# First attention of the second block: a pair's logits as one alternating run, the second pair of a step one projection tile later

## The chip, the core and the metric

The kernel runs on one core of a Trainium2 chip. The metric is the device time of one execution in microseconds (us), lower is better; the kernel before takes 1923.35 us (median of 3 runs, 1921.4 to 1927.18).

## The reference

The program computes two transformer blocks on one sequence of 512 tokens of width 1024, in float32. The first block is a gated delta net beside a retention mixer and a convolutional MLP. The second block has two layers, each an attention and a squared-ReLU MLP; the change lies in the attention of its first layer. Cut to what matters there:

```python
A_GROUPS = ((128, 1, 6), (512, 4, 5), (2048, 16, 5))     # window, dilation, heads
def dilated_window_attention(xn, w_qkv, w_o, rel_bias):  # 16 heads of 64
    q, k, v = split(xn @ w_qkv)                          # q scaled by 64 ** -0.5
    for (win, dil, nh) in A_GROUPS:
        n_side = win // (2 * dil)                        # 64 keys on either side, dil apart
        logits = q . k over the window + bias            # -inf outside the sequence
        lse = logsumexp(logits); p = exp(logits - lse); o = p . v
        glses.append(logsumexp(lse over the group's heads) - log(nh))
    alpha = softmax(glses)                               # one weight per token and group
    return concat(o * 3 * alpha) @ w_o
```

## The kernel before, in words

Activations are held with features on the 128 partitions and the 512 tokens along the free axis, as 8 tiles. Every projection of a layer is made of tiles of 128 output features: `project` issues 24 matmuls of 512 columns for one tile (8 slices of the contraction, 3 products of a high and a low half of weights and activations). They write a tile `ps_pj` of PSUM; VectorE evacuates it. The weights come by DMA in blocks of two tiles (`raw`), ScalarE copies their high half (`hi`, L251) and VectorE takes the rest (`lo`, L252). TensorE (PE), VectorE (DVE) and ScalarE (ACT) each run their own instructions in order.

`layer_a` (L988) works through a table of steps, `A_STEPS` (L26). Step numbers 0 to 3 each stand for four heads, that is two pairs: `q0`, `k0`, `v0` are two projection tiles each, `s0` the logits and the softmax of the four heads, `t0` the transposes of their probabilities, `p0` the products with v. After `s0` stands `v0` (two tiles), then `t0`; after `s1`, `s2` and `s3` stand `v1`, `q3` and `v2`, then `t1`, `t2` and `t3`. `a0` makes the weights of the three groups from all heads' minima `MN` and sums `SS`; it begins with 12 matmuls `ps_bc`.

The two heads of a pair lie in one tile of q and k, the first on partitions 0 to 63, the second on 64 to 127. A head's logits are 4 matmuls with a contraction of 64, one per block `j` of 128 queries. In the first group (heads 0 to 5) they have 192, 256, 256 and 192 columns, and two blocks share a PSUM tile `ps_lg`; in the other groups (heads 6 to 15) they have 128 columns, and all four blocks share one. The trace shows each of these float32 matmuls as two, called passes here: 128 for 64 instructions. For each block VectorE adds the bias and takes the minimum (L1083, the negated logits are kept), and ScalarE takes the exponential with its sum (L1085); per head follow a reciprocal (L1087) and the normalisation (L1090). `softmax_head` writes this block by block: matmul, addition, exponential, next block. The probabilities of the first group take one of 3 buffers `P` per head, those of the others one per pair. PSUM tiles other than `ps_pj` come from a pool `pw` of 5.

The order on each engine is made by a list scheduler when the program is built, from the order of the code, the dependencies and its own estimates; `chain` and `in_order` pin one instruction behind another. `M_["pe"]` is the last projection matmul written.

Of the kernel before, what the change touches and what calls it, by code (L numbers as in the profile page):

```python
# [9 lines left out]
F32 = mybir.dt.float32  # L10
F32R = mybir.dt.float32r
AF = mybir.ActivationFunctionType
ALU = mybir.AluOpType
# [3 lines left out]
P = 128  # L17
T = 512
# [5 lines left out]
A_GROUP = [0] * 6 + [1] * 5 + [2] * 5  # L24
# [145 lines left out]
def build(nc, tc, a, out, phases=("mix", "mlp1", "A", "mlpA", "B", "mlpB")):  # L170
# [12 lines left out]
    act = nc.scalar.activation  # L183
    V = nc.vector
    G = nc.gpsimd

    def mm(o, l, r, start=True, stop=True):
        return nc.tensor.matmul(o, lhsT=l, rhs=r, start=start, stop=stop)  # L188
# [8 lines left out]
    def in_order(i1, i2):  # L197
        tc.add_manual_dep(i2.ins, i1.ins.name, mybir.DependencyInfo(
            mybir.DependencyClass.NoSync, mybir.DependencyReason.DATA))
# [5 lines left out]
    def chain(insts):  # L205
        for x, y in zip(insts, insts[1:]):
            in_order(x, y)

    def pwt(name, shape=None):
        return pw.tile(shape or [P, T], F32, tag="w", name=name)  # L210
# [75 lines left out]
    M_ = {}  # L286
# [92 lines left out]
    def project(pieces, x, n=T, cols=P):  # L379

        if pre:
            return pre.pop(0)
        ps = pj.tile([P, T], F32, tag="pj", name="ps_pj")[0:cols, 0:n]
        nk = len(x)
        for k in range(nk):
            hi, lo = pieces[k // KD]
            M_["pe"] = mm3(ps, (hi[:, k % KD, 0:cols], lo[:, k % KD, 0:cols]), x[k], k == 0, k == nk - 1)
        return ps
# [86 lines left out]
    def mixer(st):  # L475
# [8 lines left out]
        def unit(tag, bufs, name, dt=F32, shape=None):  # L484
            pool = lp if tag == "L" else gp
            return pool.tile(shape or [P, T], dt, tag=tag, name=name, bufs=bufs)
# [79 lines left out]
        def stage_a(hh):  # L566
            H = HD[hh]
            kT, KQ, vT = H["kT"], H["KQ"], H["vT"]

# [12 lines left out]
            V.tensor_scalar(out=rq, in0=rq, scalar1=128 ** -0.5, scalar2=None, op0=ALU.mult)  # L582
            H["rq"] = rq
            brk = sp.tile([P, 4], F32, tag="brk", name="brk")
# [22 lines left out]
            G.tensor_tensor(out=qd, in0=KQ[:, 1, :], in1=er, op=ALU.mult)  # L607
            H["qd"] = qd
            kbe = unit("L", NL, "kbe")
            G.tensor_tensor(out=kbe, in0=KQ[:, 0, :], in1=er, op=ALU.mult)  # L610
            H["kbe"] = kbe
            N = unit("L", NL, "N")
            QE = unit("L", NL, "QE")
            for c2 in range(2):
# [6 lines left out]
                for aa, (o_, m_) in enumerate(((N, E2), (QE, E))):  # L621
                    V.tensor_tensor(out=o_[:, cs].rearrange("p (c i) -> p c i", c=2), in0=pg[:, :, aa, :],
                                    in1=m_[:, cs].rearrange("p (c i) -> p c i", c=2), op=ALU.mult)
            H["N"], H["QE"] = N, QE
            nc.sync.dma_start(d1[hh], N.rearrange("p (c i) -> p c i", c=4))
# [363 lines left out]
    def layer_a(st, biasd):  # L989
        x = st.x  # L990
# [3 lines left out]
        gp = tmpc.__enter__()  # L994
        b1 = gp.tile([P, 6, 256], F32, name="b1")
        b2 = gp.tile([P, 5, P], F32, name="b2")
        b3 = gp.tile([P, 5, P], F32, name="b3")
# [9 lines left out]
        MN = gp.tile([P, 16, 4], F32, name="MN")  # L1007
        SS = gp.tile([P, 16, 4], F32, name="SS")
        RC = gp.tile([P, 16, 4], F32, name="RC")
# [23 lines left out]
        def evac(ps, m, scale, dst, ordf):  # L1033
            gs = (A_GROUP[2 * m], A_GROUP[2 * m + 1])
            parts = [(slice(0, P), gs[0])] if gs[0] == gs[1] else [(slice(0, 64), gs[0]), (slice(64, P), gs[1])]
            for sl, g in parts:
                i = V.tensor_tensor(out=ordf(g, dst[sl, :]), in0=nat(g, ps[sl, :]), in1=nat(g, scale[sl, :]), op=ALU.mult)
            return i
# [11 lines left out]
            for c in range(4):  # L1050
                V.tensor_copy(b3[32 * c:32 * c + 32, :, 96 - 32 * c:128 - 32 * c], b3t[32 * c:32 * c + 32])

        PP = {}

        def softmax_head(hh, q, k):
            g = A_GROUP[hh]
            pr = slice(64 * (hh % 2), 64 * (hh % 2) + 64)
            W = 256 if g == 0 else P
            if g == 0:
                pt = gp.tile([P, 4, W], F32, tag="P", name="pt", bufs=3)  # L1060
            else:
                if hh % 2 == 0:
                    PP[hh // 2] = gp.tile([P, 2, 4, W], F32, tag="P", name="pt", bufs=3)
                pt = PP[hh // 2][:, hh % 2]
            H = dict(P=pt, rng=[])
            for j in range(4):
                if g == 0:
                    if j % 2 == 0:
                        lg = pwt("ps_lg").rearrange("p (j x) -> p j x", j=2)
                    k0, k1 = max(0, P * j - 64), min(T, P * j + 192)  # L1070
                    x0 = k0 - (P * j - 64)
                    x1 = x0 + k1 - k0
                    lj = lg[:, j % 2, x0:x1]
                    bias = b1[:, hh, x0:x1]
                else:
                    if j == 0:
                        lg = pwt("ps_lg").rearrange("p (j x) -> p j x", j=4)
                    k0, k1, x0, x1 = P * j, P * j + P, 0, P
                    lj = lg[:, j, :]
                    bias = (b2[:, hh - 6, :] if g == 1 else b3[:, hh - 11, :])  # L1080
                H["rng"].append((x0, x1))
                mm(lj, q[pr, P * j:P * j + P], k[pr, k0:k1])
                V.tensor_tensor_reduce(out=pt[:, j, x0:x1], in0=lj, in1=bias, scale=1.0, scalar=3e38,  # L1083
                                       op0=ALU.add, op1=ALU.min, accum_out=MN[:, hh, j:j + 1])
                act(out=pt[:, j, x0:x1], in_=pt[:, j, x0:x1], func=AF.Exp, scale=-1.0, bias=MN[:, hh, j:j + 1],  # L1085
                    accum_out=SS[:, hh, j:j + 1])
            V.reciprocal(out=RC[:, hh, :], in_=SS[:, hh, :])  # L1087
            for j0, j1, x0, x1 in ((0, 1, 64, 256), (1, 3, 0, 256), (3, 4, 0, 192)) if g == 0 else ((0, 4, 0, P),):
                ap = pt[:, j0:j1, x0:x1]
                V.tensor_tensor(out=ap, in0=ap, in1=RC[:, hh, j0:j1].unsqueeze(2).to_broadcast([P, j1 - j0, x1 - x0]),  # L1090
                                op=ALU.mult)
            return H

        def vtiles(m, vT):

# [100 lines left out]
        def proj(m0, nm):  # L1196
            wb = ws.take()
            r = []
            for i in range(2):
                ps = project(wb[i:i + 1], x)  # L1200
                t = gp.tile([P, T], F32, tag=nm, name=nm, bufs=2)
                M_["evac"] = evac(ps, m0 + i, rs8 if nm == "q" else st.rs, t, rorder if nm == "q" else order)
                r.append(t)
            return r

        def parts_of(m):
# [26 lines left out]
        M_["evac"] = None  # L1233
        oT, HS, qv, kv, vv = {}, {}, {}, {}, {}

        def soft_pairs(i2):
            for i in range(2):
                m = 2 * i2 + i
                HS[m] = [softmax_head(2 * m + e, qv[i2][i], kv[i2][i]) for e in range(2)]

        def turn_pairs(i2):
            for hh in range(4 * i2, 4 * i2 + 4):
# [13 lines left out]
        for step in A_STEPS:  # L1256
            nm, i2 = step[0], int(step[1])
            if step == "q1":
                load_third_bias()
            if step == "q2":  # L1260
                third_bias()
            if nm in "qkv":
                {"q": qv, "k": kv, "v": vv}[nm][i2] = proj(2 * i2, nm)
            elif nm == "s":
                soft_pairs(i2)
            elif nm == "t":
                turn_pairs(i2)
            elif nm == "p":
                pv_pairs(i2)
            else:  # L1270
                alphas()
                for m in range(4):
                    weigh(m, lambda g, sl: nat(g, oT[m][sl, :]))
# [328 lines left out]
```

## Time and profile before

| | |
|---|---|
| median of 3 runs | 1923.35 us |
| profiled execution, its own time | 1921.55 us |
| span of the profiled execution, first to last instruction | 1919.7 us |
| mean granted TensorE clock | 0.997 of full speed |
| PE busy | 1885.3 us, 98% |
| DVE, ACT, GpSimd busy | 1109.8, 766.1, 143.3 us |
| first and last logits matmul of this attention start at | 727.5 and 859.4 us |

In a page's or a view's rows, PE is a matmul on TensorE, PEld a load of its weights, and "out<-in" names the tiles. A row of the timeline gives the start in us, the time from the first start to the last end, the engine, the line and the operation, and how many instructions it merges (x4). Matmuls overlap in time, so the distance of two starts is what one costs a busy PE, and not its duration.

### The profile page before, as it was taken

Reading aid. Unit: us, or ns where it says so; the run is one execution under the profiler, and the core shown is the slowest. Engines: PE = TensorE matmul, PEld = TensorE weight load, DVE = VectorE, ACT = ScalarE, POOL = GpSimd, SP = SyncE. Lnnn points to the kernel's source line nnn. Section 1 sums busy time; section 2 is a strip of 40 time slices with the busy share of each in tenths; the row PEclk is TensorE's granted clock in tenths of the full one; section 3 lists DMA queues with packets and bytes.
Section 4 is the critical chain, followed back from the end, with each engine's and each line's share of the span. In section 5 each row is a group of like instructions: output and inputs, shape, how many; then the busy total and the mean of one; then the engine's idle time right before and its main releaser. Section 6 shows DMA issues by size and latency. Waiting matters only on the chain.

```text
span 1919.7 us, 23518 instructions
## 1 busy us (share of the span) xinstructions
PE 1885.3 (98%) x9219; PEld 1545.1 (80%) x9219; DVE 1109.8 (58%) x2109; ACT 766.1 (40%) x1350; POOL 143.3 (7%) x136
## 2 busy tenths in 40 slices
PE   7999999999999999999999999999999999999997
PEld 5887878788888887777888888888888888888886
DVE  7795756666356575558544344447877754334433
ACT  5523334343234444345342133336656543213322
POOL 1231210011001002000000000001111000000000
PEclk9999999999999999999999999999999999999999
DMA  5231213222322234112323222333222232222321
GB/s 191 79 116 56 74 45 121 95 88 88 110 103 86 76 112 160 64 52 99 110 89 109 88 106 92 111 131 135 95 73 101 81 112 88 97 101 89 109 88 44
DMA packets 39646, 185.53 MB, mean 97 GB/s; under 512 B 9055, under 2 KB 10847, under 8 KB 22000
## 3 DMA queue, kind: packets, MB, share of 16 engines
q1 hardware_dynamic: 37552, 177.45, 26.3%
q0 software_dynamic: 1984, 6.59, 1.0%
q8 instruction: 72, 1.18, 0.2%
q14 instruction: 38, 0.31, 0.1%
HBM read 176.31 MB, written 7.71 MB: 96 GB/s over the span
## 4 chain that ended last, share of the span: by engine, by line
PE 55%; DVE 3%; ACT 1%; issue 1%; DVEq 0%; ACTq 0%
PE ps_pj L188 49%; PE ps_ob L188 1%; PE ps_lgb L188 1%; PE ps_po L188 1%; PE ps_aT L1380 1%; PE ps_lg L188 1%; ACT junk L1397 0%; PE ps_bc L188 0%; DVE KL L1337 0%; DVE lo L252 0%; DVE nb L408 0%; DVE nb L409 0%; PE ps_obT L1409 0%; PE ps_pT L1140 0%; PE ps_mean L188 0%
## 5 line engine op out<-in xcount | busy, mean ns | idle before, releaser
L188 PE MATMUL ps_pj<-xh,hi 128*128 128x512 f32 x1504 | 592.2, 394 | 10.2 <-ACT hi L251 9.3
L188 PE MATMUL ps_pj<-xl,hi 128*128 128x512 f32 x1504 | 591.7, 393 | 0.0
L188 PE MATMUL ps_pj<-xh,lo 128*128 128x512 f32 x1504 | 590.9, 393 | 0.0
L251 ACT ACTIVATE hi<-raw 128x1024 fp32r<-128x1024 f32 (+2 forms) x308 | 317.2, 1031 | 649.1 <-PE ps_pj L188 611.0
L252 DVE TENSOR_TENSOR lo<-raw,hi 128x1024 fp32r<-128x1024 f32 (+2 forms) x308 | 369.6, 1202 | 300.2 <-ACT hi L251 299.2
L188 PEld LDWEIGHTS ps_pj<-xh,hi 128*128 128x128 f32 x1504 | 283.1, 188 | 69.0 <-ACT hi L251 9.8
L188 PEld LDWEIGHTS ps_pj<-xh,lo 128*128 128x128 f32 x1504 | 283.1, 188 | 58.1 <-DVE lo L252 1.1
L188 PEld LDWEIGHTS ps_pj<-xl,hi 128*128 128x128 f32 x1504 | 283.1, 188 | 57.6 <-DVE xl L280 0.6
L188 PE MATMUL ps_pj<-ah,lo 128*128 128x512 f32 (+1 forms) x704 | 271.0, 385 | 0.0
L188 PE MATMUL ps_pj<-al,hi 128*128 128x512 f32 (+1 forms) x704 | 270.7, 385 | 0.2 <-DVE al L277 0.2
L188 PE MATMUL ps_pj<-ah,hi 128*128 128x512 f32 (+1 forms) x704 | 270.9, 385 | 0.0
L188 PEld LDWEIGHTS ps_pj<-al,hi 128*128 128x128 f32 x704 | 132.3, 188 | 26.9 <-DVE al L277 0.5
L188 PEld LDWEIGHTS ps_pj<-ah,hi 128*128 128x128 f32 x704 | 132.3, 188 | 26.4 <-ACT ah L276 0.4
L188 PEld LDWEIGHTS ps_pj<-ah,lo 128*128 128x128 f32 x704 | 132.3, 188 | 25.9
L469 DVE TENSOR_TENSOR ot<-ps_pj,r 128x512 f32<-128x512 f32 x31 | 21.5, 692 | 108.1 <-PE ps_pj L188 108.1
L188 PE MATMUL ps_pj<-mh,hi 128*128 128x512 f32 x192 | 74.9, 394 | 1.0 <-ACT mh L276 0.9
L276 ACT ACTIVATE ah<-ms 128x512 fp32r<-128x512 f32 x64 | 40.4, 632 | 87.4 <-DVE ms L974 85.9
L188 PE MATMUL ps_pj<-ml,hi 128*128 128x512 f32 x192 | 74.4, 392 | 0.6 <-DVE ml L277 0.6
L188 PE MATMUL ps_pj<-mh,lo 128*128 128x512 f32 x192 | 74.0, 390 | 0.0
L277 DVE TENSOR_TENSOR al<-ms,ah 128x512 fp32r<-128x512 f32 x64 | 44.3, 693 | 45.0 <-ACT ah L276 45.0
L947 DVE SCALAR_TENSOR_TENSOR my<-ms,cols,my 128x511 f32<-128x511 f32 (+1 forms) x88 | 65.6, 748 | 2.8 <-ACT my L945 1.3
L1364 ACT ACTIVATE Lb<-Lb,bmn 128x512 f32<-128x512 f32 x64 | 45.6, 714 | 13.9 <-DVE bmn L1362 11.6
(341 smaller groups left out, 1895.9 us busy)
## 6 DMA issues: line engine op xcount, KB each, us to landing
raw<-w_all SPq DMA_DIRECT2D x137, 1024.0 KB
bt<-biasd SPq DMA_DIRECT2D x16, 448.0 KB
raw<-w_all SPq DMA_DIRECT2D x8, 768.0 KB
raw<-w_all SPq DMA_DIRECT2D x8, 640.0 KB
hscr<-h POOLq DMA_DIRECT2D x16, 256.0 KB, 2.5
hold<-hscr SPq DMA_DIRECT2D x16, 256.0 KB
hs<-x_t SPq DMA_DIRECT2D x8, 256.0 KB
hold<-x_t SPq DMA_DIRECT2D x8, 256.0 KB
```

The lines of the kernel that those rows point to most:

```text
L188: return nc.tensor.matmul(o, lhsT=l, rhs=r, start=start, stop=stop)
L251: act(out=hv, in_=iv, func=AF.Copy)
L252: i_lo = V.tensor_tensor(out=lv, in0=iv, in1=hv.bitcast(F32), op=ALU.subtract)
L276: act(out=dst_hi, in_=src, func=AF.Copy)
L277: V.tensor_tensor(out=dst_lo, in0=src, in1=dst_hi.bitcast(F32), op=ALU.subtract)
L469: V.tensor_tensor(out=t, in0=ps, in1=scale_row, op=ALU.mult)
L947: V.scalar_tensor_tensor(out=y[:, jj:], in0=s[:, :T - jj], scalar=col(base + m), in1=y[:, jj:], op0=ALU.mult, op1=ALU.add)
L1364: act(out=L, in_=L, func=AF.Exp, scale=-1.0, bias=mn[:, j, t:t + 1], accum_out=ss[:, j, t:t + 1])
L1380: nc.tensor.transpose(ps[:, t * P:(t + 1) * P], A[t][:, kt * P:(kt + 1) * P], ident)
```

## The change

`softmax_head` is replaced by `softmax_pair`, for both heads of a pair. It writes the matmuls of the two heads in turn (block 0 of the first head, block 0 of the second, block 1 of the first, ...), chains them, pins the first of them behind the last projection matmul, and writes the additions and exponentials behind the matmuls of the two PSUM tiles that they read, one per head. The second pair of a step is not issued at `s`: it is kept in `second` and issued by `proj` after the next projection tile. No operand, shape, number of instructions or DMA changes.

```diff
-        def softmax_head(hh, q, k):
+        def softmax_pair(m, q, k):
+            g = A_GROUP[2 * m]
             W = 256 if g == 0 else P
+            nj = 2 if g == 0 else 4
...
-            for j in range(4):
...
-                mm(lj, q[pr, P * j:P * j + P], k[pr, k0:k1])
-                V.tensor_tensor_reduce(out=pt[:, j, x0:x1], in0=lj, in1=bias, scale=1.0, scalar=3e38,
-                                       op0=ALU.add, op1=ALU.min, accum_out=MN[:, hh, j:j + 1])
-                act(out=pt[:, j, x0:x1], in_=pt[:, j, x0:x1], func=AF.Exp, scale=-1.0, bias=MN[:, hh, j:j + 1],
-                    accum_out=SS[:, hh, j:j + 1])
+            before = M_["pe"]
+            for j0 in range(0, 4, nj):
+                lg = [pwt("ps_lg").rearrange("p (j x) -> p j x", j=nj) for _ in range(2)]
+                todo, seq = [], []
+                for j in range(j0, j0 + nj):
...
+                    for e in range(2):
+                        hh = 2 * m + e
+                        pr = slice(64 * e, 64 * e + 64)
...
+                        lj = lg[e][:, j - j0, x0:x1]
+                        Hs[e]["rng"].append((x0, x1))
+                        seq.append(mm(lj, q[pr, P * j:P * j + P], k[pr, k0:k1]))
+                        if before is not None:
+                            in_order(before, seq[0])
+                            before = None
+                        todo.append((hh, j, pts[e][:, j, x0:x1], lj, bias))
+                chain(seq)
+                for hh, j, pj_, lj, bias in sorted(todo, key=lambda t: t[:2]):
+                    V.tensor_tensor_reduce(out=pj_, in0=lj, in1=bias, scale=1.0, scalar=3e38,
+                                           op0=ALU.add, op1=ALU.min, accum_out=MN[:, hh, j:j + 1])
+                    act(out=pj_, in_=pj_, func=AF.Exp, scale=-1.0, bias=MN[:, hh, j:j + 1],
+                        accum_out=SS[:, hh, j:j + 1])
...
                 M_["evac"] = evac(ps, m0 + i, rs8 if nm == "q" else st.rs, t, rorder if nm == "q" else order)
                 r.append(t)
+                if second:
+                    soft_pair(*second.pop())
...
+        second = []
+
+        def soft_pair(i2, i):
+            HS[2 * i2 + i] = softmax_pair(2 * i2 + i, qv[i2][i], kv[i2][i])
+
         def soft_pairs(i2):
-            for i in range(2):
-                m = 2 * i2 + i
-                HS[m] = [softmax_head(2 * m + e, qv[i2][i], kv[i2][i]) for e in range(2)]
+            soft_pair(i2, 0)
+            second.append((i2, 1))
```

What this does to the order is shown at three places. The first is PE at step `s0`, where the first pair's logits stand. `q_5949` and `k_6013` are the first pair's q and k. Before, heads 0 and 1 have the PSUM tiles 6043, 6050 and 6062, 6069 (blocks 0 and 1, blocks 2 and 3); what stands in brackets is the engine whose counter the matmul waits for:

```order
L188 MATMUL ps_lg_6043<-k_6013,q_5949 128x192 [waits DVE_49]
L188 MATMUL ps_lg_6050<-k_6013,q_5949 128x256
L188 MATMUL ps_lg_6062<-k_6013,q_5949 128x192 [waits PE_49]
L188 MATMUL ps_lg_6069<-k_6013,q_5949 128x256 [waits Activation_49]
L188 MATMUL ps_lg_6043<-k_6013,q_5949 128x256 [waits DVE_49]
L188 MATMUL ps_lg_6050<-k_6013,q_5949 128x192 [waits DVE_49]
L188 MATMUL ps_lg_6062<-k_6013,q_5949 128x256 [waits DVE_49]
L188 MATMUL ps_lg_6069<-k_6013,q_5949 128x192 [waits DVE_49]
```

The same place in the changed kernel; the tiles are 6044, 6058 (head 0) and 6045, 6059 (head 1), and `ps_pj_6090` is the first tile of `v0`:

```order
L188 MATMUL ps_lg_6044<-k_6013,q_5949 128x192 [waits DVE_49]
L188 MATMUL ps_lg_6045<-k_6013,q_5949 128x192
L188 MATMUL ps_lg_6044<-k_6013,q_5949 128x256
L188 MATMUL ps_lg_6045<-k_6013,q_5949 128x256
L188 MATMUL ps_lg_6058<-k_6013,q_5949 128x256 [waits PE_49]
L188 MATMUL ps_lg_6059<-k_6013,q_5949 128x256 [waits Activation_49]
L188 MATMUL ps_lg_6058<-k_6013,q_5949 128x192
L188 MATMUL ps_lg_6059<-k_6013,q_5949 128x192
L188 MATMUL ps_pj_6090<-xh0_5425,hi_5980 128x512 [waits PE_49]
```

The waits of the second half for VectorE are gone, the two heads alternate, and projection matmuls follow at once, where before the second pair's logits followed.

The second place is PE at step `s3`, heads 12 to 15 (128 columns). Before, the logits of both pairs (`q_6898` and `q_6925`) mix with each other and with the first projection matmuls of `v2` (`ps_pj_7091`):

```order
L188 MATMUL ps_lg_7020<-k_6990,q_6898 128x128 [waits DVE_49]
L188 MATMUL ps_pj_7091<-xh0_5425,lo_6958 128x512
L188 MATMUL ps_lg_7035<-k_6990,q_6898 128x128 [waits DVE_49]
L188 MATMUL ps_lg_7051<-k_7017,q_6925 128x128 [waits DVE_49]
L188 MATMUL ps_pj_7091<-xh1_5477,hi_6957 128x512
L188 MATMUL ps_lg_7066<-k_7017,q_6925 128x128 [waits DVE_49]
L188 MATMUL ps_pj_7091<-xl1_5478,hi_6957 128x512
L188 MATMUL ps_pj_7091<-xh1_5477,lo_6958 128x512
L188 MATMUL ps_pj_7091<-xh2_5530,hi_6957 128x512
L188 MATMUL ps_lg_7066<-k_7017,q_6925 128x128 [waits DVE_49]
```

Changed, the second pair's run stands whole between the 24 matmuls of the first tile of `v2` (`ps_pj_7060`) and the 24 of the second (`ps_pj_7118`), after which the transposes of `t3` come:

```order
L188 MATMUL ps_pj_7060<-xh7_5795,lo_6958 128x512
L188 MATMUL ps_lg_7088<-k_7017,q_6925 128x128 [waits DVE_49,Activation_49]
L188 MATMUL ps_lg_7089<-k_7017,q_6925 128x128 [waits Activation_49]
L188 MATMUL ps_lg_7088<-k_7017,q_6925 128x128
L188 MATMUL ps_lg_7089<-k_7017,q_6925 128x128
L188 MATMUL ps_lg_7088<-k_7017,q_6925 128x128
L188 MATMUL ps_lg_7089<-k_7017,q_6925 128x128
L188 MATMUL ps_lg_7088<-k_7017,q_6925 128x128
L188 MATMUL ps_lg_7089<-k_7017,q_6925 128x128
L188 MATMUL ps_pj_7118<-xh0_5425,hi_6961 128x512 [waits PE_49]
```

All eight of a pair's matmuls now stand together, and the two logits runs of a step are 24 projection matmuls apart.

The third place is VectorE at the same step, from the first reciprocal on. Before (`pt_7019` are the probabilities of heads 12 and 13, `pt_7050` those of 14 and 15; `v_7116` is the evacuation of the first tile of `v2`):

```order
L1087 RECIPROCAL RC_5905<-SS_5904 128x4 [waits Activation_49]
L1083 ISA pt_7050,MN_5903<-ps_lg_7066,b3_5898 128x128 [waits PE_49]
L1083 ISA MN_5903 128x1
L1090 TENSOR_TENSOR pt_7019<-pt_7019,RC_5905 128x512 [waits DVE_49]
L1087 RECIPROCAL RC_5905<-SS_5904 128x4 [waits Activation_49]
L252 TENSOR_TENSOR lo_7084<-raw_7081,hi_7083 128x1024 [waits DMAHW2_49]
L1090 TENSOR_TENSOR pt_7050<-pt_7050,RC_5905 128x512 [waits DVE_49]
L1087 RECIPROCAL RC_5905<-SS_5904 128x4 [waits Activation_49]
L252 TENSOR_TENSOR lo_7088<-raw_7081,hi_7087 128x1024
L1090 TENSOR_TENSOR pt_7050<-pt_7050,RC_5905 128x512 [waits DVE_49]
L1037 TENSOR_TENSOR v_7116<-ps_pj_7091,rs_5864 128x128x4 [waits PE_49]
```

Changed (`pt_7087` are heads 14 and 15, `v_7085` is the first tile of `v2`):

```order
L1096 RECIPROCAL RC_5905<-SS_5904 128x4 [waits Activation_49]
L252 TENSOR_TENSOR lo_7057<-raw_7050,hi_7056 128x1024
L1099 TENSOR_TENSOR pt_7019<-pt_7019,RC_5905 128x512 [waits DVE_49]
L1096 RECIPROCAL RC_5905<-SS_5904 128x4 [waits Activation_49]
L1099 TENSOR_TENSOR pt_7019<-pt_7019,RC_5905 128x512 [waits DVE_49]
L1037 TENSOR_TENSOR v_7085<-ps_pj_7060,rs_5864 128x128x4 [waits PE_49]
L1090 ISA pt_7087,MN_5903<-ps_lg_7088,b3_5898 128x128 [waits PE_49]
L1090 ISA MN_5903 128x1
```

The second pair's additions now come behind the evacuation of the first tile of v, where before they were mixed with the first pair's.

## Rows read from the trace of the kernel before

**Rows 1.** The page: span, and busy time by engine with share and instructions.
```profile
span 1919.7 us, 23518 instructions
PE 1885.3 (98%) x9219; PEld 1545.1 (80%) x9219; DVE 1109.8 (58%) x2109; ACT 766.1 (40%) x1350; POOL 143.3 (7%) x136
```

**Rows 2.** The logits' tile ps_lg: instructions, then idle time before them by releaser.
```profile
L188 PE MATMUL ps_lg<-k,q x128: 269/323/480, 727.5 to 859.4; 64*128 64x128 f32 x80, 64*128 64x192 f32 x24, 64*128 64x256 f32 x24
...
  DVE MN L1083: 6.5, 19
```

**Rows 3.** Stretches around logits (start:end, length, busy by engine, PEclk), first, some, last.
```profile
727.17:732.14 4.97, 4.57 (x29) 3.01 (x28) 4.55 (x20) 4.68 (x13) 3.06 (x4) 1.00 1.06 390
733.99:735.16 1.17, 1.17 (x5) 0.59 (x4) 1.17 (x5) 1.07 (x5) 0.00 (x0) 1.00 0.12 39
...
852.53:853.60 1.07, 1.07 (x7) 0.60 (x6) 0.65 (x1) 0.82 (x1) 0.00 (x0) 1.00 0.00 0
853.60:858.59 4.99, 4.71 (x32) 3.25 (x30) 3.97 (x33) 4.62 (x23) 0.00 (x0) 1.00 0.01 2
858.82:859.90 1.08, 1.08 (x6) 0.59 (x4) 0.76 (x5) 1.08 (x7) 0.00 (x0) 1.00 0.05 15
sum 31.85, PE 30.51 PEld 19.11 DVE 26.54 ACT 26.82 POOL 3.06; mean PE 2.03 PEld 1.27 DVE 1.77 ACT 1.79 POOL 0.20
```

**Rows 4.** Chain of waits: two projection tiles without anything between.
```profile
842.02 10.91 PE ps_pj L188 x48
```

**Rows 5.** Timeline of PE at step s3.
```profile
852.85 0.49 PE L188 MATMUL ps_lg<-k,q 64*128 64x128 f32 x4
...
857.84 0.49 PE L188 MATMUL ps_lg<-k,q 64*128 64x128 f32 x2
```

**Rows 6.** Timeline of PE at step s0: wider logits.
```profile
731.17 0.70 PE L188 MATMUL ps_lg<-k,q 64*128 64x256 f32 x4 [0.31 <-DVE MN L1083]
...
734.30 0.59 PE L188 MATMUL ps_lg<-k,q 64*128 64x192 f32 x2
```

**Rows 7.** Timeline of PE: a pair's products with v, two heads in turn.
```profile
812.92 0.40 PE L188 MATMUL ps_pj<-xh,hi 128*128 128x512 f32 x1
813.25 1.09 PE L188 MATMUL ps_po<-pT,vt 128*64 128x128 f32 x16
814.27 0.50 PE L188 MATMUL ps_pj<-xl,hi 128*128 128x512 f32 x1
814.60 0.39 PE L188 MATMUL ps_pj<-xh,lo 128*128 128x512 f32 x1
```

**Rows 8.** Timeline of PE, 727.4 to 728.4 us: the first eight logits passes.
```profile
727.49 1.03 PE L188 MATMUL ps_lg<-k,q 64*128 64x192 f32 x8
```

**Rows 9.** Timeline of VectorE at step s3: the four heads' softmax.
```profile
853.89 0.27 DVE L1083 CUSTOM_DVE_ANT_0 pt<-ps_lg,b 128x128 f32<-128x128 f32 x1
...
862.38 1.19 DVE L252 TENSOR_TENSOR lo<-raw,hi 128x1024 fp32r<-128x1024 f32 x1
863.49 0.69 DVE L1090 TENSOR_TENSOR pt<-pt,RC 128x512 f32<-128x512 f32 x1
864.09 1.09 DVE L1037 TENSOR_TENSOR v<-ps_pj,rs 128x512 f32<-128x512 f32 x1
865.01 0.18 DVE L1167 TENSOR_REDUCE mg<-MN 128x4 f32<-128x20 f32 x1
```

**Rows 10.** Timeline of ScalarE: the sums' logarithm in step a0.
```profile
867.01 0.21 ACT L1174 ACTIVATE sg<-sg 128x12 f32<-128x12 f32 x1
```

**Rows 11.** Timeline of PE at steps t3 and a0.
```profile
868.77 0.39 PE L188 MATMUL ps_pj<-xh,lo 128*128 128x512 f32 x1
869.00 1.91 PE L1140 MATMUL ps_pT<-ident,pt 128*128 128x128 f32 x16
870.74 2.84 PE L188 MATMUL ps_bc<-ident,sg 128*128 128x128 f32 x24
```

**Rows 12.** Timeline of PE at step t0: the smaller runs of transposes.
```profile
744.82 0.47 PE L188 MATMUL ps_pj<-xh,hi 128*128 128x512 f32 x1
745.26 0.66 PE L1129 MATMUL ps_pT<-ident,pt 128*128 128x128 f32 x4
745.67 0.48 PE L188 MATMUL ps_pj<-xl,hi 128*128 128x512 f32 x1
```

**Rows 13.** Waits on PE that stand behind step a0.
```profile
PE ps_pj L188 <- ACT mh L276: 0.9, 1, 0.9
PE ps_pj L188 <- DVE ml L277: 0.6, 1, 0.6
```

**Rows 14.** Timeline of PE's weight loads where the tile shape changes.
```profile
762.72 0.20 PEld L188 LDWEIGHTS ps_po<-pT,vt 64*64 64x64 f32 x4 [0.17 <-issue]
```

More of the change, by code (lines that the diff above doesn't have):

```diff
@@ L1051, in third_bias @@
                 V.tensor_copy(b3[32 * c:32 * c + 32, :, 96 - 32 * c:128 - 32 * c], b3t[32 * c:32 * c + 32])
-        PP = {}
-        def softmax_head(hh, q, k):
-            g = A_GROUP[hh]
-            pr = slice(64 * (hh % 2), 64 * (hh % 2) + 64)
+        def softmax_pair(m, q, k):
+            g = A_GROUP[2 * m]
             W = 256 if g == 0 else P
+            nj = 2 if g == 0 else 4
             if g == 0:
-                pt = gp.tile([P, 4, W], F32, tag="P", name="pt", bufs=3)
+                pts = [gp.tile([P, 4, W], F32, tag="P", name="pt", bufs=3) for _ in range(2)]
@@ L1061, in softmax_head @@
             else:
[L1062 to L1065, printed above, removed]
-            for j in range(4):
[L1067 to L1071, printed above, removed]
-                    x1 = x0 + k1 - k0
[L1073 to L1081, printed above, removed]
-                mm(lj, q[pr, P * j:P * j + P], k[pr, k0:k1])
-                V.tensor_tensor_reduce(out=pt[:, j, x0:x1], in0=lj, in1=bias, scale=1.0, scalar=3e38,
-                                       op0=ALU.add, op1=ALU.min, accum_out=MN[:, hh, j:j + 1])
-                act(out=pt[:, j, x0:x1], in_=pt[:, j, x0:x1], func=AF.Exp, scale=-1.0, bias=MN[:, hh, j:j + 1],
-                    accum_out=SS[:, hh, j:j + 1])
@@ L1087, in softmax_head @@
[L1087 to L1092, printed above, removed]
+                pt2 = gp.tile([P, 2, 4, W], F32, tag="P", name="pt", bufs=3)
+                pts = [pt2[:, e] for e in range(2)]
@@ new lines, in softmax_pair @@
+            Hs = [dict(P=pts[e], rng=[]) for e in range(2)]
+            before = M_["pe"]
[3 more added lines that the diff above has]
+                for j in range(j0, j0 + nj):
+                    if g == 0:
+                        k0, k1 = max(0, P * j - 64), min(T, P * j + 192)
+                        x0 = k0 - (P * j - 64)
+                    else:
+                        k0, k1, x0 = P * j, P * j + P, 0
+                    x1 = x0 + k1 - k0
+                    for e in range(2):
+                        hh = 2 * m + e
+                        pr = slice(64 * e, 64 * e + 64)
+                        gh = A_GROUP[hh]
+                        bias = b1[:, hh, x0:x1] if gh == 0 else b2[:, hh - 6, :] if gh == 1 else b3[:, hh - 11, :]
+                        lj = lg[e][:, j - j0, x0:x1]
[11 more added lines that the diff above has]
+                        accum_out=SS[:, hh, j:j + 1])
@@ new lines, in softmax_pair @@
+            for e in range(2):
+                hh, pt = 2 * m + e, pts[e]
+                V.reciprocal(out=RC[:, hh, :], in_=SS[:, hh, :])
+                for j0, j1, x0, x1 in ((0, 1, 64, 256), (1, 3, 0, 256), (3, 4, 0, 192)) if g == 0 else ((0, 4, 0, P),):
+                    ap = pt[:, j0:j1, x0:x1]
+                    V.tensor_tensor(out=ap, in0=ap,
+                                    in1=RC[:, hh, j0:j1].unsqueeze(2).to_broadcast([P, j1 - j0, x1 - x0]), op=ALU.mult)
+            return Hs
```

## The prediction

> **What bounds the kernel.** I first read the page's engine times: PE is busy for 1885.3 of 1919.7 us, VectorE for 58% and ScalarE for 40% [rows 1]. The reader is to see there that only time taken from PE's own stream shortens the program. Then the view of the tile ps_lg: this attention's logits are 128 passes of 64 rows, and PE's side sat idle for 6.5 us in front of them, in 19 places, until VectorE had read an earlier block [rows 2]. That is little, so I asked what the logits cost PE in all. I cut 15 stretches out of the trace, each from the last projection matmul before some logits to the second one after them; together they hold all 128 passes and take 31.85 us [rows 3]. Most hold two projection matmuls, the stretch 853.60 to 858.59 four and the one from 825.09 to 830.39 five, 13 x 2 + 4 + 5 = 35. An undisturbed one costs 10.91 / 48 = 0.227 us [rows 4], so 35 x 0.227 = 7.9 us are projections, and **the logits cost PE 23.9 us**, waits and changes of shape included. In these stretches the granted clock is 1.00 of full speed, the 2.4 GHz level, so no clock is to be won.
>
> **What one pass costs, and that a second head rides free.** At step s3 one row shows four passes of 128 columns, two heads with two each, in 0.49 us; another shows two passes of one head alone, also in 0.49 us [rows 5]. Two heads on the two halves of the array therefore run side by side, if both are there. I call the time of such a pair of passes a slot. Two slots of 128, 192 and 256 columns take 0.49, 0.59 and 0.70 us [rows 5, 6]: 64 columns more cost two slots 0.105 us, so a slot is 0.105, 0.158 and 0.21 us wide, and 0.28 us are a fixed start and end.
>
> Before, many passes ran alone: blocks of one head waited for VectorE, and the other head's had been done or were not yet released. The order listing of step s3 shows single logits strewn among projections; each such place pays the changes of shape again.
>
> **The change, part by part.** (1) *Logits in turn, in one run.* A pair becomes 8 slots in one stretch. For 128 columns: the stretch 852.53 to 853.60 has two slots and costs 1.07 - 2 x 0.227 = 0.62 us [rows 3]; six slots more make 0.62 + 6 x 0.105 = 1.25 us. A run of the same form confirms it: the products with v, two heads in turn, 16 passes of 128 columns, go from 812.92 to 814.60, 1.68 - 0.45 = 1.23 us [rows 7]. For the first group: the stretch 733.99 to 735.16 has two slots of 192 and costs 1.17 - 0.45 = 0.72 us [rows 3]; two more of 192 and four of 256 make 0.72 + 0.32 + 0.84 = 1.88 us. Five pairs are of the first kind, three of the second: 5 x 1.25 + 3 x 1.88 = 11.9 us. **23.9 - 11.9 = 12.0 us less.** Waits inside a run are not added: the listings keep a counter only where a run takes a PSUM tile anew, and those were read long before.
>
> Here a rule can be weighed. The first eight passes after 727.49 us take 1.03 us [rows 8], though the listing before has blocks of 192 and 256 columns of head 0 ahead of head 1's: 0.28 + 2 x 0.158 + 2 x 0.21 = 1.02 us, the time of heads side by side from the first pass on. The Trainium skill ("TensorE: Matmul & The Clock Gate", Part 3, "What overlaps and what doesn't") says that matmuls start and end strictly in the program's order. By that rule head 1 would have begun beside head 0's last pass, and the eight would have taken 0.28 + 2 x 0.74 - 0.21 = 1.55 us; the trace disagrees. If the rule held in the new run, its two passes of one head would pair with a shift, 9 slots for 8, 5 x 0.105 + 3 x 0.158 = 1.0 us more, and the sum below would end at 1910.7 for 1909.7, inside the forecast's range.
>
> (2) *The second pair one projection tile later.* It moves no work to PE. It parts what PE waited for: the additions of the first pair are done while the tile's 24 matmuls run (24 x 0.227 = 5.45 us). What is late next are the transposes, which now stand 24 projection matmuls behind the second pair's logits. Four heads of step s3 took VectorE and ScalarE from 853.89 to 864.18 us, with two weight splits among them [rows 9], so a pair needs about 5.1 us; in front of it stands now the evacuation of v, 1.09 us [rows 9]. Those 6.2 us are covered by the run (about 0.9), the tile (5.45) and the first two heads' transposes (half of 1.74 us [rows 11]), 7.2 us. I cost it at nothing; without the cover every microsecond would be paid at four steps. Step a0 follows: before, its last small operation on ScalarE ended at 867.2 and ps_bc started at 870.74 us [rows 10, 11]. Its chain, from the first reduction at 865.01 on, takes 2.2 us to that row and about 0.3 us more, so it would be ready 6.2 + 2.5 = 8.7 us after the second pair's start, against 0.9 + 5.45 + 1.74 = 8.1 us: 0 to 0.6 us of wait. I take 0, because the listing lets its first operations run among the normalisations. The waits behind a0 (0.9 and 0.6 us [rows 13]) hang on VectorE's work after ps_bc and stay.
>
> (3) *Transposes of step t0.* They were five runs and become six, since the first group has three probability buffers and head 3 must wait for head 0's. A short run of four costs 0.85 us from projection to projection [rows 12], 0.23 of it the projection and 0.43 its transposes (16 take 870.74 - 869.00 = 1.74 us [rows 11]): 0.2 us more.
>
> VectorE, ScalarE, the DMA queues and GpSimd keep their instructions; weights are split about three tiles (16 us) before PE takes them, since four buffers each hold one tile, so a split that moves by a few microseconds is hidden.
>
> **Sum.** 12.0 - 0.2 = 11.8 us off the profiled execution's own time of 1921.55 us: 1909.7. The median of the runs shown is 1.8 us above that execution; I forecast **1910.5 us**, inside that offset. What a measurement of this kernel tells from no change is about 0.3%, 5.8 us.
>
> **Rivals.**
> *The heads do not ride side by side in the new run* (that the change does not do what it says): alternating matmuls would then be 16 solo slots. 128 columns: the solo stretch 858.82 to 859.90 costs 0.63 us [rows 3], plus 14 x 0.105 is 2.10; the first group 0.72 + 6 x 0.158 + 8 x 0.21 = 3.35. 5 x 2.10 + 3 x 3.35 = 20.6 us, a gain of 3.3 - 0.2: 1918.5 us, no change that can be told. Against it stand [rows 5, 7, 8].
> *The transposes wait.* If two weight splits (1.19 us each [rows 9]) fall into the second pair's 5.1 us, the chain is 8.6 us against 7.2: 1.4 us at each of four steps, 5.6 us, and 0.6 at a0. 1911.5 to 1917 us. For it: at s0 head 3 holds two of the five PSUM tiles until head 0 is transposed. Against it: VectorE was idle for 42% of the span [rows 1], and at t3 the transposes started 0.23 us after the last projection matmul, without a wait [rows 11].
> *Slower: the half of the array costs a switch.* Where the tile shape changes between matmuls of one run, the weight load sat idle for 0.17 us [rows 14]. If going from rows 0 to 63 to rows 64 to 127 cost that too and forbade overlap, the 7 alternations of each of 8 runs cost 56 x 0.17 = 9.5 us on top of the first rival: 1928 us. It decides from 3.1 / 56 = 0.055 us per alternation on. Four passes of two heads in 0.49 us [rows 5] speak against it.
>
> **Chances and range.** Forecast 0.78; no overlap 0.08; transposes wait 0.10, of which 0.07 stay below the bound of 1915.8 us (1921.55 - 5.8); switch 0.04. Faster 0.78 + 0.07 = 0.85, same 0.08 + 0.03 = 0.11, slower 0.04. The range goes up to 1917, which takes in the waiting transposes and leaves out the other two (0.12). Downwards no term has room beyond 12.0 us; 1909.5 less 2 us, about what the runs before differ by downwards from their median, gives 1907.5.
>
> **What would show it.** In the profile after: eight runs of 16 logits passes, 8 slots each, about 1.1 us (128 columns) and 1.75 us (first group) from first start to last end; eight stretches with an excess of 1.2 to 1.3 and 1.8 to 1.9 us; no idle time before ps_lg released by VectorE; the first ps_pT of each step without a wait; no wait of ps_bc for VectorE. Wrong it would be if a run of 16 passes took over 2 us, or if PE sat idle for over 1 us before the transposes of a step.

## The result, and the profile after

The changed kernel takes 1912.18 us (median of 20 executions, 1909.17 to 1927.51), the kernel before, run beside it, 1925.04 us (median of 20, 1919.87 to 1936.42). The ratio, which is not simply that of the two medians (0.9933), is 0.9949 with a 95% interval from 0.9931 to 0.9966: **faster by 0.5%**, 6.5 to 13 us. The forecast was 1910.5 us.

Whole times differ by up to 18 us between executions of one kernel, and with them goes the mean granted clock, from 0.998 down to 0.988 (the last section shows one place where it falls). Where it was 0.997 or more, 11 executions of the changed kernel have a median of 1911.4 us. Of 19 executions of the kernel before, run beside the first experiments, 8 were at 0.997 or more; their median is 1922.5 us, 11.1 us above.

For single microseconds another measure is better. In the nine traces of this study the clock is lowered only far ahead of this attention or in the last microseconds of the program. A second attention follows, whose logits write the tile `ps_lgb`; between the two the granted clock is 1.00 throughout. So I take **the distance from the first start of ps_lg to the first start of ps_lgb**. The row of ps_lgb in the view of that tile, before:

```profile
L188 PE MATMUL ps_lgb<-KH,Q x64: 388/393/504, 1311.5 to 1489.5; 128*128 128x512 f32 x64
```

and after:

```profile
L188 PE MATMUL ps_lgb<-KH,Q x64: 388/393/501, 1301.7 to 1479.7; 128*128 128x512 f32 x64
```

Before, the distance is 1311.49 - 727.49 = 584.0 us, after 1301.69 - 729.10 = 572.6 us: **11.4 us less** in the one execution that each trace holds. From the first ps_lgb to the end all nine traces agree within 0.16 us (608.11 to 608.27), which says how finely such a distance can be read.

The page after, to be held against [rows 1]:

```profile
span 1910.0 us, 23525 instructions
...
PE 1875.1 (98%) x9219; PEld 1541.2 (81%) x9219; DVE 1110.6 (58%) x2109; ACT 765.3 (40%) x1350; POOL 143.1 (7%) x136
```

PE is busy for 10.2 us less with the same 9219 records of matmuls; the other engines are where they were. The span falls by 9.7 and not by 11.4 us, because the changed kernel's profiled execution reached this attention 1.6 us later (729.10 for 727.49 us): its first wait for weights, in code that the change doesn't touch, was 11.0 us long where two such waits had been 9.3 us together.

The tile ps_lg after, with the idle time in front of it, to be held against [rows 2]:

```profile
L188 PE MATMUL ps_lg<-k,q x128: 272/272/427, 729.1 to 853.4; 64*128 64x128 f32 x80, 64*128 64x192 f32 x24, 64*128 64x256 f32 x24
...
its engine sat idle before it (us, times) until:
  issue: 2.8, 8
```

The idle time released by VectorE is gone. What is left is eight times 0.35 us of the weight load, once at the head of each run, where the tile shape changes; the view names nothing that it waited for. The starts show directly what the change was made for: before, 58 of the 128 passes start with no pass of the other head within 40 ns; after, none does, and the 128 passes start as 64 pairs.

The stretches around the logits after (the columns are those of [rows 3]):

```profile
728.78:731.15 2.37, 2.37 (x19) 1.70 (x18) 1.94 (x2) 2.09 (x2) 2.37 (x3) 1.00 0.97 294
736.20:738.57 2.37, 2.37 (x19) 1.70 (x18) 2.34 (x7) 1.06 (x1) 0.00 (x0) 1.00 0.74 209
775.32:777.69 2.37, 2.37 (x19) 1.70 (x18) 1.94 (x2) 1.06 (x1) 0.00 (x0) 1.00 0.00 0
782.74:784.49 1.75, 1.75 (x20) 1.27 (x18) 1.75 (x7) 1.06 (x1) 0.00 (x0) 1.00 0.83 295
...
852.23:853.98 1.75, 1.75 (x19) 1.27 (x18) 1.73 (x5) 1.06 (x1) 0.00 (x0) 1.00 0.84 257
sum 15.86, PE 15.86 PEld 11.43 DVE 14.03 ACT 10.07 POOL 2.37; mean PE 1.98 PEld 1.43 DVE 1.75 ACT 1.26 POOL 0.30
```

Eight stretches stand where fifteen stood, three of 2.37 and five of 1.75 us, PE busy in all of them to the end. Each holds two projection matmuls; 15.86 - 16 x 0.227 = 12.2 us is what the logits cost PE now, against 23.9 before.

One such run in PE's timeline after, and the place where the transposes of t3 and step a0 follow, to be held against [rows 11]:

```profile
782.74 0.39 PE L188 MATMUL ps_pj<-xh,lo 128*128 128x512 f32 x1
783.06 1.16 PE L188 MATMUL ps_lg<-k,q 64*128 64x128 f32 x16
784.15 0.50 PE L188 MATMUL ps_pj<-xh,hi 128*128 128x512 f32 x1
...
858.99 0.39 PE L188 MATMUL ps_pj<-xh,lo 128*128 128x512 f32 x1
859.23 1.91 PE L1149 MATMUL ps_pT<-ident,pt 128*128 128x128 f32 x16
860.97 0.61 PE L188 MATMUL ps_bc<-ident,sg 128*128 128x128 f32 x4
```

Sixteen passes take 1.16 us. The transposes start 0.24 us after the last projection matmul and ps_bc 1.74 us after them, as before to the hundredth: nothing waits there.

### The profile page after: what moved, and what is told of

Read it like the earlier page. It is cut to its first block, busy times and chain, and to the rows that moved or that the text cites. A ratio compares the mean times of both kernels' runs of the same rounds, so it can differ in the third digit from the quotient of the medians.

```text
span 1910.0 us, 23525 instructions
## 1 busy us (share of the span) xinstructions
PE 1875.1 (98%) x9219; PEld 1541.2 (81%) x9219; DVE 1110.6 (58%) x2109; ACT 765.3 (40%) x1350; POOL 143.1 (7%) x136
## 4 chain that ended last, share of the span: by engine, by line
PE 55%; DVE 3%; ACT 1%; issue 1%; DVEq 0%; ACTq 0%
PE ps_pj L188 49%; PE ps_ob L188 1%; PE ps_lgb L188 1%; PE ps_po L188 1%; PE ps_aT L1396 1%; ACT junk L1413 0%; PE ps_lg L188 0%; DVE lo L252 0%; PE ps_bc L188 0%; DVE KL L1353 0%; DVE nb L408 0%; DVE nb L409 0%; PE ps_obT L1425 0%; PE ps_pT L1149 0%; PE ps_mean L188 0%
```

## Experiments

**A ledger for the logits.** It needs a price for a slot and one for a stretch, and one kernel gives both: both heads' logits are computed from the first head's 64 partitions, on one half of the array, so that no two passes can lie side by side.

```diff
-                        pr = slice(64 * e, 64 * e + 64)
+                        pr = slice(0, 64)
```

> The changed kernel with both heads' logits computed from the first head's 64 partitions, so all passes lie on one half of the array and cannot ride side by side; the second head's logits are then not its own. Order, waits and bytes are those of the changed kernel. Theory (side by side is worth 8 slots a run): 16 slots for 8, 5 x 8 x 0.105 + 3 x (4 x 0.158 + 4 x 0.21) = 4.2 + 4.4 = 8.6 us more, distance 581.2 us; runs of 16 passes take about 2.0 and 3.2 us. Rival (the gain is the waits and the joined runs alone, overlap gives nothing): 572.6 to 574 us.

Measured: a distance of 581.6 us. Its stretches, of the first group and of 128 columns:

```profile
736.35:740.23 3.88, 3.88 (x19) 3.06 (x18) 3.45 (x7) 2.80 (x5) 3.08 (x4) 1.00 0.98 346
794.83:797.47 2.64, 2.64 (x20) 2.15 (x18) 1.15 (x6) 1.18 (x2) 0.00 (x0) 1.00 0.58 239
```

Less two projection matmuls these are 3.43 and 2.18 us, where the changed kernel has 1.92 and 1.29. Sixteen passes in single file against eight pairs: eight slots more cost 2.18 - 1.29 = 0.89 us, 0.111 each, and 1.51 us, 0.189 each as a mean over 192 and 256 columns. What remains of a run is 1.29 - 0.89 = 0.40 and 1.92 - 1.51 = 0.41 us, nearly the same in both: **the fixed price of a stretch**, taken as 0.41. Side by side is worth 9.0 us of the distance, 581.6 against 572.6; 581.2 was expected.

With these two prices every trace's excess splits into stretches x 0.41 us, the 64 slots that cannot be saved (40 x 0.111 + 24 x 0.189 = 8.95 us), and a rest, which is passes that ran alone, pauses, and returns within a stretch. The prices come from the changed kernel and the one on one half, so the changed kernel's rest of 0.0 is so by construction; the other rows are what the ledger tells:

| kernel | distance, us | excess, us | stretches x 0.41 | rest |
|---|---|---|---|---|
| before | 584.0 | 23.9 | 15: 6.2 | 8.8 |
| changed | 572.6 | 12.2 | 8: 3.3 | 0.0 |
| in turn, both pairs together | 576.5 | 16.3 | 4: 1.6 | 5.7 |
| in turn, joined in steps 2 and 3 only | 573.6 | 13.3 | 6: 2.5 | 1.9 |
| second pair later, not in turn | 588.4 | 28.1 | 20: 8.2 | 11.0 |
| blocks four and four | 575.6 | 15.2 | 8: 3.3 | 3.0 |
| blocks two and two | 573.1 | 12.7 | 8: 3.3 | 0.5 |

Of the 8.8 us before, PE's pauses are 31.85 - 30.51 = 1.3 [rows 3]. The kernels of the lower rows follow one by one; the last experiment is not among them, since transposes share its stretches.

**The runs in turn alone.** The second pair's run is issued at once behind the first pair's.

```diff
         def soft_pairs(i2):
             soft_pair(i2, 0)
-            second.append((i2, 1))
+            soft_pair(i2, 1)
```

> The changed kernel with the second pair issued at once (both pairs of a step at s), so the first part of the change alone. Measure: the distance from the first logits of this attention to the first logits of the second attention's ps_lgb, 584.0 us before and 572.6 us changed. Theory (PE pays for slots and changes of shape): the two runs of a step join; at steps 2 and 3 this saves one change of shape each, about 0.43 us, at steps 0 and 1 the second run waits for PSUM tiles (4 + 4 and 4 + 2 of 5), 0.5 to 1.5 us each. Distance 572 to 575 us, so nearly the whole gain of 11.4 us. Rival (the later second pair is what frees PE from VectorE): the waits come back, 579 to 584 us.

Measured: 1915.29 us (median of 10), ratio 0.9947 [0.9918, 0.9976] to the kernel before; distance 576.5 us, 1.5 us past the upper end of what was expected and short of the rival's 579. PE's timeline, at the four steps:

```profile
726.43 2.10 PE L188 MATMUL ps_lg<-k,q 64*128 64x192 f32 x18
729.90 2.26 PE L188 MATMUL ps_lg<-k,q 64*128 64x192 f32 x14 [1.36 <-DVE MN L1090]
...
774.93 2.00 PE L188 MATMUL ps_lg<-k,q 64*128 64x192 f32 x18
777.84 1.16 PE L188 MATMUL ps_lg<-k,q 64*128 64x128 f32 x14 [0.91 <-DVE MN L1090]
...
819.83 1.71 PE L188 MATMUL ps_lg<-k,q 64*128 64x128 f32 x18
822.19 1.13 PE L188 MATMUL ps_lg<-k,q 64*128 64x128 f32 x14 [0.66 <-DVE k L1037]
...
847.01 1.16 PE L188 MATMUL ps_lg<-k,q 64*128 64x128 f32 x16
848.33 1.16 PE L188 MATMUL ps_lg<-k,q 64*128 64x128 f32 x16 [0.17 <-DVE k L1037]
```

At each step PE stops in or before the second pair's run: at s0 and s1 until VectorE has read a PSUM tile of the first pair, which the second wants, and at s2 and s3 until VectorE has evacuated the second pair's k. The matmuls idle for 1.36 + 0.91 + 0.66 + 0.17 = 3.1 us. Where the two heads of the second pair do not get their tiles or their k at the same time, passes run alone again: 18 of the 128 by the same count of starts, which is 4 slots of 0.111 and 5 of 0.189, 1.4 us. That makes 4.5 of the rest of 5.7 us; the other 1.2 were not taken apart. Four stretches fewer than in the changed kernel give back 1.6. **The runs of `softmax_pair` without the move are worth 7.5 us of distance, and the later second pair another 3.9 on top of it.** The runs differ from before by their order, the chain, the pin behind the last projection matmul and the additions written behind them; only the order was tried apart (below). The ratios of whole times, 0.9947 here and 0.9949 for the change, cannot tell these 3.9 us; the distances and the waits can.

**Joined in two steps, apart in two.** To see that the second pair's waits are each step's own, the pairs of steps 0 and 1 stand apart as in the change, those of 2 and 3 together.

```diff
-            second.append((i2, 1))
+            if i2 < 2:
+                second.append((i2, 1))
+            else:
+                soft_pair(i2, 1)
```

> The second pair later at steps 0 and 1 as in the change, both pairs together at steps 2 and 3. Same measure. Theory (with both pairs together, PE waits at the second pair for VectorE's additions or for its k, and that costs more than the separate run's own fixed part): the joined stretches of steps 2 and 3 cost 3.6 and 2.6 us as in the run with all four joined, against 2 x 1.295 = 2.59 us each: 572.6 + 1.0 + 0.0 = 573.7 us. Rival (the gain of the later pair lies in the first two steps alone, whose softmax is longer; joined runs of 128 columns save a change of shape): 571.5 to 572.3 us.

Measured: 573.6 us. Its two joined stretches:

```profile
824.40:828.48 4.08, 3.36 (x36) 2.53 (x35) 3.56 (x6) 1.06 (x1) 0.00 (x0) 1.00 0.01 2
851.58:854.65 3.07, 2.90 (x35) 2.27 (x34) 2.65 (x7) 1.34 (x2) 0.00 (x0) 1.00 0.03 8
```

4.08 and 3.07 us less 0.45 are 3.6 and 2.6, as in the run with all four joined. At s3, where only 0.17 us was waited, joining is even with two separate runs (2 x 1.29 = 2.6); at no step is it cheaper.

**The later second pair alone.** Heads one by one with `softmax_head` as before, which `soft_pair` calls here for both heads; the second pair is kept until after the next projection tile, as in the change.

```diff
...
+                if second:
+                    soft_pair(*second.pop())
...
         def soft_pairs(i2):
-            for i in range(2):
-                m = 2 * i2 + i
-                HS[m] = [softmax_head(2 * m + e, qv[i2][i], kv[i2][i]) for e in range(2)]
+            soft_pair(i2, 0)
+            second.append((i2, 1))
```

> The kernel before with its softmax written head by head, and only the second pair of a step moved one projection tile later: the second part of the change alone. Distance as above. Theory (slots and shapes): logits of one pair still wait block by block for VectorE, passes of one head run alone, and there are more stretches than before (18 to 20 for 15), so nothing is gained: 583 to 589 us, about 0 to 5 us slower than before. Rival (the delay frees PE): 573 to 578 us.

Measured: 1928.28 us (median of 10), ratio 1.0012 [0.9984, 1.004]; distance 588.4 us, 4.4 more than before and within what was expected; the whole times cannot be told from before. A piece of PE's timeline at the second pair of s3:

```profile
868.60 0.49 PE L188 MATMUL ps_lg<-k,q 64*128 64x128 f32 x4
869.02 0.50 PE L188 MATMUL ps_pj<-xh,hi 128*128 128x512 f32 x1
869.36 0.39 PE L188 MATMUL ps_pj<-xl,hi 128*128 128x512 f32 x1
869.59 0.40 PE L188 MATMUL ps_pj<-xh,lo 128*128 128x512 f32 x1
870.00 0.49 PE L188 MATMUL ps_lg<-k,q 64*128 64x128 f32 x2
870.41 0.50 PE L188 MATMUL ps_pj<-xh,hi 128*128 128x512 f32 x1
870.85 0.48 PE L188 MATMUL ps_lg<-k,q 64*128 64x128 f32 x2
```

Written block by block, the second pair finds more projections to scatter among, and PE pays for 20 stretches, 15 of them with four passes only, in place of 15 in all. The same move gains 3.9 us behind runs in turn and loses 4.4 without them.

**The order of the blocks.** Within a PSUM tile first all of one head's blocks, then all of the other's: two and two in the first group, four and four with 128 columns.

```diff
-                chain(seq)
+                chain(seq[0::2] + seq[1::2])
```

> The changed kernel with the run's order alone altered: first all blocks of one head in the two PSUM tiles at hand, then those of the other (128 columns: four and four; first group: two and two, twice), chained in that order. Theory (the two halves of the array take their matmuls independently of each other, as the first eight passes of the kernel before did): runs as in the changed kernel, 1.1 and 1.75 us for 16 passes, distance 572.6 us within 0.5. Rival (matmuls start strictly in the program's order): only passes at the seam overlap; a run of 128 columns has 15 slots for 8, 0.74 us more, one of the first group 13 or 14 for 8, about 1.0 us more: 5 x 0.74 + 3 x 1.0 = 6.7 us, 579 us.

Measured: 575.6 us, between the two expectations, so neither holds. The stretches of the first group and of 128 columns:

```profile
728.12:730.59 2.47, 2.47 (x19) 1.85 (x18) 2.04 (x2) 2.19 (x2) 2.47 (x3) 1.00 1.03 335
782.25:784.54 2.29, 2.29 (x20) 1.81 (x18) 2.29 (x10) 1.11 (x2) 0.00 (x0) 1.00 0.81 322
```

Two and two costs 2.02 us for 1.92, almost nothing more; four and four 1.84 for 1.29, five slots more. The passes' starts say why. Of the 16 passes from 782.56 us on, this is the view of the tile cut at 783.10 us (the passes that start before):

```profile
L188 PE MATMUL ps_lg<-k,q x4: 272/272/373, 782.6 to 783.0; 64*128 64x128 f32 x4
```

Four start alone; the fifth and another start within 5 ns of each other, at 783.113 and 783.118 us, and from there on the two heads run side by side, but for one slot, until the first one is through. The passes start at 13 distinct moments in place of 8. The view does not name the heads; that the other one is the second head's first pass is read from its length, 373 ns, which in the run in turn at 783.06 us only the first pass of each head has (the others have 272). It thus started together with the fifth, while three more of the first head stood ahead of it in the program. It was pulled ahead, but not from eight places back.

A new theory, then: a pass of the other half starts up to four places ahead of its turn. It says that two and two is almost free with 128 columns too, which was tried by itself, with the first group in turn as in the change:

```diff
-                chain(seq)
+                chain([seq[x] for x in (0, 2, 1, 3, 4, 6, 5, 7)] if nj == 4 else seq)
```

> The five pairs with 128 columns are issued as two blocks of the first head, two of the second, two of the first, two of the second, in place of one and one; the first group stays in turn. Same measure. Theory (a pass of the other half of the array starts up to four places ahead of its turn, as in the run with four and four, where the second head's first pass started beside the first head's fifth): all eight slots but one are filled, an excess of 1.3 to 1.4 us per run, 572.6 to 573.2 us in all. Rival (passes start ahead only beside a wider pass, or no more than two places): two to four slots more per run, 1.5 to 1.7 us, 573.6 to 574.7 us.

Measured: 573.1 us, and each of the five stretches of 128 columns as this one:

```profile
779.70:781.55 1.85, 1.85 (x20) 1.37 (x19) 1.85 (x7) 1.06 (x1) 0.00 (x0) 1.00 0.85 319
```

1.85 - 0.45 = 1.39 us, one slot of 0.1 more than in turn: as the theory had it.

**One tile later still.** The second pair stands behind both projection tiles, directly in front of the transposes, so that no tile lies between it and them.

```diff
-                if second:
-                    soft_pair(*second.pop())
...
+            if second and nm != 'k':
+                soft_pair(*second.pop())
```

> The second pair of a step one projection tile later still, that is after both tiles and directly in front of the step's transposes; the runs stay in turn. Measure: the distance from the first start of ps_lg to the first start of ps_lgb, 584.0 us before, 572.6 us changed. Theory (the tile behind the second pair's logits is cover for its 6.2 us of softmax): the cover goes, so the transposes of heads 2 and 3 stand in pieces behind only 3 to 25 projection matmuls; some seven more pieces at 0.2 us are 1.4 us, and one to two of the four steps wait 1 to 2 us for VectorE or ScalarE: 574.5 to 578 us, with waits of ps_pT in the list. Rival (how late the second pair stands does not matter, once the first pair's tiles have been read): 572 to 573.5 us, no wait of ps_pT.

Measured: 578.2 us, 5.7 more than the change and 0.2 past the upper end of what was expected; 1921.25 us (median of 10), ratio 0.9972 [0.9946, 0.9998] to the kernel before. Four waits of PE are in its list that the changed kernel's does not have (us in total, times, longest):

```profile
PE ps_po L188 <- ACT vt L1120: 1.8, 2, 1.0
...
PE ps_pT L1138 <- DVE MN L1090: 1.3, 2, 1.0
PE ps_pT L1149 <- DVE dm L1177: 1.2, 1, 1.2
...
PE ps_bc L188 <- DVE sg L1185: 1.1, 1, 1.1
```

They sum to 5.4 us, but not all of that is the softmax. PE's busy time over the whole distance, in the changed kernel and here:

```profile
729.10:1301.69 572.59, 570.15 (x2789) 1.00 0.29 103
735.52:1313.76 578.24, 571.12 (x2788) 1.00 0.29 102
```

PE's idle time rises from 2.4 to 7.1 us, 4.7 of the 5.7; the other 1.0 is busy time, in a stream whose transposes stand in other pieces, and was not taken apart. The waits of ps_pT and ps_bc, 1.3 + 1.2 + 1.1 = 3.6 us, are the softmax that the tile had covered: at the transposes of s1 and s3 above all, and in step a0; at s2 PE does not wait. The two of ps_po stand in p3, behind a0:

```profile
889.55 1.06 ACT L251 ACTIVATE hi<-raw 128x1024 fp32r<-128x1024 f32 x1 [2.73 <-PE ps_pj L188]
890.52 0.58 ACT L1120 ACTIVATE vt<-ps_v 128x512 f32<-128x512 f32 x1
...
891.15 1.09 PE L188 MATMUL ps_po<-pT,vt 128*64 128x128 f32 x16 [1.02 <-ACT vt L1120]
```

There ScalarE copies weights ahead of the transposed v. It is another order of p3, not the second pair's softmax; the two waits of [rows 13], 1.5 us before, are 0.7 here.

## Why the prediction was right, point by point

*Logits in one run* (term 1: 12.0 us). Measured 23.9 - 12.2 = 11.7. The method held: a stretch counted against undisturbed projections, slots from rows of two passes each. Its sizes were a little low: 1.29 and 1.92 us per run for 1.25 and 1.88, since a slot inside a run is 0.111 us wide and not 0.105. Eight runs make 0.3 us of it. The two marks named beforehand, about 1.1 and 1.75 us from first start to last end, came out as 1.16 and 1.78.

*No waits inside a run.* True, but the reason given was too short. "Those were read long before" holds for the second pair only because a projection tile stands in front of it; with both pairs together PE stopped at every step. So point 2, "It moves no work to PE. It parts what PE waited for", and the cost of nothing that went with it, were right for the sum only because term 1 had already assumed eight separate runs without waits: the later pair is what makes that assumption true, and 3.9 of the 11.4 us hang on it. At steps 2 and 3 it was not a PSUM tile that PE waited for but the second pair's k, a wait that the prediction does not name.

*The cover of the transposes* (7.2 us against a chain of 6.2). It holds: no wait of ps_pT, and ps_bc directly behind the transposes. From the first start of the second pair's logits to the end of its normalisation the chain took 6.1, 6.9 and 5.7 us at s1, s2 and s3 (at s0 head 3 waits for a probability buffer, and its transposes are a run of their own). The longest, at s2, where the logits start at 826.38 us:

```profile
832.56 0.69 DVE L1099 TENSOR_TENSOR pt<-pt,RC 128x512 f32<-128x512 f32 x1
...
833.06 1.91 PE L1149 MATMUL ps_pT<-ident,pt 128*128 128x128 f32 x16
```

It ends at 833.25 us, and the transposes of this pair, the second half of the row, begin at about 833.9: the cover is 7.5 us there and 0.7 is left. The evacuation of v, counted into the chain at 1.09 us, runs beside the logits at s3 (852.66 to 853.73, run from 852.55 to 853.71). The chain of step a0, forecast as 6.2 + 2.5 = 8.7 us, took 6.7: its reductions ran between the normalisations, as the prediction had it for taking 0 of its 0 to 0.6 us, and its last operation ended at 859.29 us, ps_bc started at 860.97. The last experiment shows that the cover works and is needed: without the tile 5.7 us come back, 3.6 of them as waits for the softmax, in sum and not at each step.

*Transposes of t0* (0.2 us). They are six runs, as the listing had them. Logits save 11.7 and the distance 11.4; the 0.3 us between hold this term and all else.

*The start of the argument.* The 6.5 us of idle time in [rows 2] were read as PE's side in front of the logits. Split by engine, 5.4 of them are the weight loads' and only 1.0 the matmuls'. Nothing in the sum rested on it; the sum rested on the stretches. The range's lower end, too, starts from 1909.5 where the sum has 1909.7, which changes nothing.

*Rivals.* Heads that don't ride side by side would have been the kernel with one half only: its 21.2 us of excess are close to the 20.6 forecast for that rival. A switch between halves would show between their starts: in a run in turn the two heads' passes start 7 ns apart, and 0.055 us per alternation would have decided. Waiting transposes did not come.

*The order of matmuls.* The Trainium skill ("TensorE: Matmul & The Clock Gate", Part 3, "What overlaps and what doesn't") has matmuls start and end strictly in the program's order. By that rule two and two with 128 columns would have needed 13 slots for 8 (three overlaps among 16 passes), 0.41 + 13 x 0.111 = 1.85 us; the trace has 1.39 and disagrees, as [rows 8] did. For runs in turn the prediction priced the rule at one slot more per run, 1.0 us in all; the trace has 64 pairs of starts, eight slots per run, so it disagrees there too, but the change tests it by that one microsecond only.

## What to carry to other kernels

When PE is the bound, cut its timeline into stretches between two neighbours of the common kind and subtract those neighbours: busy shares hide what short matmuls of another shape cost, here 23.9 us of PE for 9.0 us of slots. Write work that can lie side by side on two halves of the array next to each other in the program, in turn or two and two, and give the next such run enough other work in front of it that its PSUM tiles have been read and its operands are there; one of the two alone brought 7.5 us or lost 4.4, together they brought 11.4. Before moving work later, count what then lies between it and its first reader: one tile was cover enough here, with 0.7 us to spare at one step, and none cost half of the gain.

## What the runs showed that was not expected

**Matmuls on the two halves of the array pass each other, but not far.** With eight passes of one head ahead of the other's, the other's first pass started with the fifth; with four ahead, 13 ns after the first. Both, and two and two, fit a reach of four places; whether it is counted in passes or bounded by something else was not tried. So "each run their own instructions in order", as the kernel before is described, is not exact for TensorE.

**A clock that falls ahead of the attention in some executions and not in others.** The windows of PE from 245 to 250 and from 250 to 270 us (the third figure group is PEclk), in the run with the second pair behind both tiles:

```profile
245.00:250.00 5.00, 5.00 (x44) 1.00 0.00 0
250.00:270.00 20.00, 19.80 (x163) 0.57 0.15 54
```

and in the changed kernel:

```profile
245.00:250.00 5.00, 5.00 (x42) 1.00 0.00 0
250.00:270.00 20.00, 19.80 (x204) 1.00 0.15 54
```

The granted clock was 0.57 of full speed on the mean there, the 1.2 GHz level for most of the 20 us, and the first logits came at 735.5 us in place of 729.1. In both traces PE was busy throughout the 5 us before, and the program up to there is the same; what decides is not in the trace. It is not the only place: in the run with steps 2 and 3 joined the clock was 0.70 on the mean from 160 to 180 us, and 1.00 from 250 to 270. For whoever measures 0.5%: compare a distance that begins behind such a stretch, or executions with equal clock.
